# Third products of the delta rule's inverse by transposes, grouped exponentials, 42 slots and other planner durations in a two-layer hybrid network

## The chip, the cores and the metric

The kernel runs on one core of a Trainium2 chip. The metric is device time in microseconds (us): the median of several executions, from the first to the last instruction with what lies around them. A profile comes from one execution of its own.

## What is computed

A network of two layers on x of shape [256, 1024] in float32. Each layer is a SwiGLU feed-forward block (FFN, hidden width 2816), a mixer, and a second FFN; behind each stands a layer norm (LN) over the scaled residual. The mixer of layer 0 joins a gated delta rule (8 heads, chunks of 64) with an mLSTM (4 heads). The mixer of layer 1 is a chunked state-space model, SSD, with 32 heads in 4 groups.

```python
for l in range(DEPTH):
    x = layer_norm(DN_ALPHA * x + 0.5 * swiglu(x, pre_gate[l], pre_up[l], pre_down[l]))
    x = layer_norm(DN_ALPHA * x + (hybrid_mixer(x) if l % 2 == 0 else ssd_mixer(x)))
    x = layer_norm(DN_ALPHA * x + 0.5 * swiglu(x, post_gate[l], post_up[l], post_down[l]))
...
# delta rule, per head and chunk of 64
lower = jnp.where(strict, einsum('bhncd,bhnjd->bhncj', kb, k) * decay, 0.0)
sol = triangular_solve(lower + eye, rhs, left_side=True, lower=True)
...
# SSD, per chunk and head
seg = jnp.exp(jnp.where(causal, a_cum[..., :, None] - a_cum[..., None, :], -jnp.inf))
y_diag = einsum('bngcj,bngrcj,bnjgrp->bncgrp', cb, seg, xdt)
d_end = jnp.exp(a_cum[..., -1:] - a_cum)
```

## The kernel before, in words

**Matmuls in three parts.** Every weight arrives by DMA as a float32 tile `raw` (mostly 512 KB). ACT (ScalarE) casts it to a rounded `hi`, DVE (VectorE) writes `lo` = raw - hi, and the activations are split alike (`xh`, `xl`). A product is three matmuls: hi with xh, lo with xh, hi with xl. The FFNs take most of the span and are made of nothing else.

**An order written ahead.** No engine chooses its next instruction at run time. The whole network is first recorded as operations in a `Plan`. `Plan.rank` gives each a due time from TensorE's (PE's) sequence, `Plan.order` walks through modelled time and puts them in a fixed sequence for each of the five queues (PE, DVE, ACT, POOL, SP; SP issues the DMAs), and `Plan.emit` writes the instructions out. So almost every row of the profile has one line, that of the emitting loop (L488). The durations of the model are in `_cost`; `HAND` and `LAG` are delays between engines, `MARGIN` a reserve for DMAs of weights; `order` also models the row of DMAs and charges ACT for a change of its function table. `plan.group()` makes one operation of several calls, `plan.behind(op)` holds an operation behind another in the plan alone.

**Buffers.** SBUF tiles come from pools: `m4` (40 slots of 128 x 1040 floats) holds raw, hi, lo and most large tiles; `m2`, `m1` and the `tiny` ones are smaller. PSUM's 8 banks have three kinds: `acc` 4, `gu` 2, `tr` 2.

**Delta rule.** `Ls` (one tile per half of the sequence) holds the lower triangles. Their 16 x 16 diagonal blocks go through a scratch array in DRAM (`scrdl`) into `ab`; `block_inverse` inverts them on DVE, with constants for a 16 x 16 identity and a strict lower triangle, and its results return through DRAM as `T` (transposed inverse) and `U` (inverse). Two levels (`lv` 0: 16 to 32 rows; `lv` 1: 32 to 64) then grow them, in 4 steps for each level (two halves, two quads `q`). A step computes YZ from U and Ls, then corrects `uu` (U) with T·YZ and `tt` (T) with YZ·T, each by four matmuls into PSUM and a subtraction on DVE. While the blocks are on their way, PE works at the projections of the hybrid mixer and at the mLSTM, whose outputs `my` it transposes (`tr<-ident,my`).

**SSD.** For each of four groups, `decays` builds two tiles `abc` (one for each half, 128 x 1024): a DMA from scratch, 8 Relu on ACT, one exponential; and `sde`, a small exponential. The convolution's outputs `cv` go through Silu on ACT (to `bf`, `cf`, `xf`), the gate `zs` too; Exp and Silu are in different function tables, and each change is an ACT_TABLE_LOAD. `xe` (DVE) and `hst` (ACT) feed the products of the states.

Of the kernel before, what the change touches and what calls it, by code (L numbers as in the profile page):

```python
# [12 lines left out]
F32 = mybir.dt.float32  # L13
# [19 lines left out]
NSLOT = 40  # L33
# [7 lines left out]
C_EYE16 = 896  # L41
C_LOW16 = 1152
C_N = 1408


def _const_array():
    i = np.arange(P)[:, None]
    j = np.arange(P)[None, :]
    c = np.zeros((P, C_N), np.float32)
    c[:, C_NEG:C_NEG + P] = np.where(i <= j, 0.0, -BIG)  # L50
    c[:, C_POS:C_POS + P] = np.where(i <= j, 0.0, BIG)
    for n, s in enumerate((16, 32)):
        c[:, C_LEV + n * P:C_LEV + n * P + P] = (i // (2 * s) == j // (2 * s)) & (i % (2 * s) < s) & (j % (2 * s) >= s)
    c[:, C_PAIR:C_PAIR + P] = i // 64 == j // 64
    c[:, C_CAU:C_CAU + P] = i <= j
    c[:, C_LOW16:C_LOW16 + 256] = np.tril(np.ones((16, 16), np.float32), -1).reshape(1, 256)
    c[:, C_EYE16:C_EYE16 + 256] = np.eye(16, dtype=np.float32).reshape(1, 256)
    return c


SB_SLOTS = {"m4": (NSLOT, WMAX), "m2": (6, 512), "m1": (6, 256), "tiny": (12, 16), "tiny96": (12, 96)}
# [12 lines left out]
class Buf:  # L74


    def __init__(self, n, tag, shape, dtype, name):
# [6 lines left out]
        self.ops = []  # L84
        self.place = None
# [99 lines left out]
class Plan:  # L185
# [83 lines left out]
    def _cost(self, op, method, a, k):  # L269
# [12 lines left out]
        elif q == "SP":  # L282
# [5 lines left out]
            op.rate = 410 if isinstance(src, bass.AP) and not src.tensor.name.startswith("scr") else 300  # L288
        else:
# [20 lines left out]
            elif q == "ACT":  # L310
                op.busy += 180 + .85 * n + 60 * scal - LAG["ACT"] + (186 if "accum_out" in k else 0)
# [38 lines left out]
    MARGIN, LEAD = 1000, 0  # L350
# [3 lines left out]
    def order(self):  # L354
# [18 lines left out]
        dma = 0.0  # L373
# [12 lines left out]

        def start(o, q):
            t = max(ready[o, q], clock[q])
            if o.news:
# [23 lines left out]
        while len(out) < len(ops):  # L413
            best = None
            for q in QUEUES:
# [4 lines left out]
                now = [(o.prio + 2 * switch(o, q), o.n, t, o) for t, o in can if t <= t0]  # L420
                mine = min(now)
                for p, n, t, o in sorted((o.prio + 2 * switch(o, q), o.n, t, o) for t, o in can if t > t0):
# [34 lines left out]
            o.done, o.begun, o.on = end, t, q  # L457
            out.append(o)
# [32 lines left out]
class Net:  # L491
# [92 lines left out]
    def consts(self):  # L584
# [7 lines left out]
        self.ones = self.one([32, S], F32, name="ones")  # L592
        nc.gpsimd.memset(self.ones, 1.0)
# [277 lines left out]
    def hyb(self, g, b, last=False):  # L871
# [24 lines left out]
        ones = self.ones[0:8]  # L896

# [38 lines left out]
        with hp():  # L936
            sin = t96(12, "sin")
            V.tensor_copy(sin[:, :, 0:8], gt[:, :, 8:16])
            V.tensor_scalar_mul(sin[:, :, 8:12], gt[:, :, 20:24], -1.0)
# [147 lines left out]
        mq = self.m4([P, 2, S], nm="mq")  # L1087
# [3 lines left out]
        mk = self.m4([P, 2, S], nm="mk")  # L1091
# [3 lines left out]
        for pr in range(2):  # L1095
            for q in range(2):
# [64 lines left out]
        with hp():  # L1161
# [8 lines left out]
            for lv in range(2):  # L1170
# [112 lines left out]
    def block_inverse(self, ab, c, dd):  # L1283
# [4 lines left out]
        eye3 = c[:, C_EYE16:C_EYE16 + 256].rearrange("p (a b) -> p a b", a=16)  # L1288
        V.tensor_mul(ab, ab, c[:, C_LOW16:C_LOW16 + 256].rearrange("p (a b) -> p a b", a=16))
# [57 lines left out]
    def ssd(self, g, b, last=False):  # L1347
# [17 lines left out]
        ones = self.ones[:, 0:P]  # L1365
# [25 lines left out]
        V.tensor_copy(flat(dt), sp)  # L1391
# [7 lines left out]
        rw = self.m1([NH, S], nm="srow")  # L1399
        ds_ = [self.scratch([NH, P], f"ds{half}") for half in range(2)]  # L1400
# [16 lines left out]
        def decays(gi):  # L1417
            for half in range(2):
# [10 lines left out]
                A.activation(bc, bc, AF.Exp, scale=-1.0)  # L1429
                M[gi, half] = bc  # L1430

# [143 lines left out]
def _layouts(i):  # L1575
    f = lambda a: np.ascontiguousarray(np.asarray(a))
    o = {"cst": _const_array(), "ident": np.eye(P, dtype=np.float32), "x": f(i["x"])[0]}
# [59 lines left out]
```

## Time and profile before

| | |
|---|---|
| median of 3 runs | 1147.33 us (1146.54 to 1148.89) |
| profiled execution, its own time | 1146.67 us |
| its span, first to last instruction | 1144.9 us |
| PE busy, of the span | 1112.7 us, 97% |
| DVE busy | 758.5 us, 66% |
| ACT busy | 587.9 us, 51% |
| mean granted TensorE clock | 0.995 |

What happens in the profiled execution is told in its own time; 1.8 us of it lie outside the span. Busy shares are means over stages with different limits. The stages by the span's clock: FFN to 182 us, hybrid mixer to 376, two FFNs with an LN between them to 730, SSD to 970, the last FFN to the end.

### The profile page before, as it was taken

Reading aid. Unit: us, or ns where it says so; the run is one execution under the profiler, and the core shown is the slowest. Engines: PE = TensorE matmul, PEld = TensorE weight load, DVE = VectorE, ACT = ScalarE, POOL = GpSimd, SP = SyncE. Lnnn points to the kernel's source line nnn. Section 1 sums busy time; section 2 is a strip of 40 time slices with the busy share of each in tenths; the row PEclk is TensorE's granted clock in tenths of the full one; section 3 lists DMA queues with packets and bytes.
Section 4 is the critical chain, followed back from the end, with each engine's and each line's share of the span. In section 5 each row is a group of like instructions: output and inputs, shape, how many; then the busy total and the mean of one; then the engine's idle time right before and its main releaser. Section 6 shows DMA issues by size and latency. Waiting matters only on the chain.

```text
span 1144.9 us, 19783 instructions
## 1 busy us (share of the span) xinstructions
PE 1112.7 (97%) x8118; PEld 1041.5 (91%) x8118; DVE 758.5 (66%) x1242; ACT 587.9 (51%) x890; POOL 26.2 (2%) x53
## 2 busy tenths in 40 slices
PE   7999999998999999999999999999999999999996
PEld 7999998998998999999899999899998779999995
DVE  6945456787969955455865545696788889655425
ACT  6755443593423544344354444379889636444410
POOL 0000000000000000000000000000011220000000
PEclk9999999998999999999999999999999999999999
DMA  9766554648424555565465555465545446655601
GB/s 358 288 212 205 196 183 133 191 171 214 186 102 159 197 190 192 191 206 174 148 223 200 188 197 187 134 217 187 185 146 178 149 163 243 218 172 187 212 19 37
DMA packets 75955, 210.02 MB, mean 183 GB/s; under 512 B 13580, under 2 KB 26328, under 8 KB 75864
## 3 DMA queue, kind: packets, MB, share of 16 engines
q1 hardware_dynamic: 75864, 208.76, 54.3%
q8 instruction: 63, 1.03, 0.4%
q14 instruction: 28, 0.23, 0.1%
HBM read 204.23 MB, written 4.50 MB: 182 GB/s over the span
## 4 chain that ended last, share of the span: by engine, by line
PE 81%; DVE 8%; ACT 6%; DMA 3%; issue 1%; SPq 0%; DVEq 0%; ACTq 0%
PE gu L488 46%; PE acc L488 32%; PE tr L488 3%; DVE cv L488 2%; DMA raw<-in_wgu 2%; DVE lo L488 2%; ACT L488 2%; ACT abc L488 1%; DVE x L488 1%; ACT cv L488 1%; DMA ab<-scrdl 1%; ACT Ls L488 1%; ACT hi L488 0%; DVE ry L488 0%; DMA x<-in_x 0%
## 5 line engine op out<-in xcount | busy, mean ns | idle before, releaser
L488 DVE TENSOR_TENSOR lo<-raw,hi 128x1024 fp32r<-128x1024 f32 (+2 forms) x358 | 428.8, 1216 | 145.0 <-ACT hi L488 141.4
L488 ACT CAST hi<-raw 128x1024 fp32r<-128x1024 f32 (+2 forms) x358 | 370.1, 1045 | 203.0 <-DMA raw<-in_wgu 125.1
L488 PE MATMUL gu<-xl,hi 128*128 128x256 f32 x1216 | 341.9, 281 | 0.0
L488 PE MATMUL gu<-xh,hi 128*128 128x256 f32 x1216 | 341.2, 281 | 0.0
L488 PE MATMUL gu<-xh,lo 128*128 128x256 f32 x1216 | 341.1, 281 | 0.0
L488 PEld LDWEIGHTS gu<-xh,hi 128*128 128x128 f32 x1216 | 229.0, 188 | 1.0
L488 PEld LDWEIGHTS gu<-xl,hi 128*128 128x128 f32 x1216 | 228.9, 188 | 1.1
L488 PEld LDWEIGHTS gu<-xh,lo 128*128 128x128 f32 x1216 | 229.1, 188 | 0.0
L488 PE MATMUL acc<-hi,h 128*128 128x512 f32 (+1 forms) x748 | 228.7, 381 | 0.0
L488 PEld LDWEIGHTS acc<-hi,h 128*128 128x128 f32 x748 | 138.1, 188 | 27.5
L488 PE MATMUL acc<-lo,h 128*128 128x512 f32 (+1 forms) x374 | 142.1, 380 | 0.0
L488 ACT ACTIVATE sg<-gu 128x256 f32<-128x256 f32 (+1 forms) x100 | 35.9, 359 | 183.3 <-PE gu L488 183.1
L488 DVE TENSOR_TENSOR hf<-sg,gu 128x256 f32<-128x256 f32 (+1 forms) x100 | 38.7, 388 | 108.2 <-ACT sg L488 108.0
L488 PE MATMUL acc<-xh,hi 128*128 128x256 f32 x320 | 92.7, 290 | 0.0
L488 PE MATMUL acc<-xl,hi 128*128 128x256 f32 x320 | 90.5, 283 | 0.0
L488 PE MATMUL acc<-xh,lo 128*128 128x256 f32 x320 | 90.2, 282 | 0.0
L488 PEld LDWEIGHTS acc<-lo,h 128*128 128x128 f32 x374 | 70.3, 188 | 13.1
L488 PE MATMUL acc<-hi,xh 128*128 128x260 f32 x224 | 64.0, 286 | 0.0
L488 PE MATMUL acc<-hi,xl 128*128 128x260 f32 x224 | 63.4, 283 | 0.4 <-DVE xl L488 0.4
L488 PE MATMUL acc<-lo,xh 128*128 128x260 f32 x224 | 63.3, 283 | 0.0
L488 PEld LDWEIGHTS acc<-xh,hi 128*128 128x128 f32 x320 | 61.0, 190 | 0.6 <-issue 0.2
L488 DVE TENSOR_TENSOR h<-hf,h 128x256 fp32r<-128x256 f32 x76 | 32.3, 425 | 44.0 <-ACT h L488 44.0
(272 smaller groups left out, 1445.5 us busy)
## 6 DMA issues: line engine op xcount, KB each, us to landing
raw<-in_wgu SPq DMA_DIRECT2D x176, 512.0 KB, 5.0
raw<-in_wd SPq DMA_DIRECT2D x88, 512.0 KB, 5.8
raw<-in_ssd_fm SPq DMA_DIRECT2D x24, 512.0 KB, 5.7
raw<-in_ssd_tm SPq DMA_DIRECT2D x16, 520.0 KB, 4.5
raw<-in_hyb_fm SPq DMA_DIRECT2D x16, 512.0 KB, 5.2
raw<-in_ssd_out SPq DMA_DIRECT2D x16, 512.0 KB, 5.7
raw<-in_hyb_tm SPq DMA_DIRECT2D x12, 520.0 KB, 4.4
raw<-in_hyb_out SPq DMA_DIRECT2D x8, 512.0 KB, 6.8
```

The source lines that it names most:

```text
L488: getattr(engines[o.on], method)(*map(real, a), **{x: real(v) for x, v in k.items()})
```

## The change

- `m4` has 42 slots instead of 40. To make room, the constants lose their two 16 x 16 tables (1408 to 896 columns), which become an array of their own, `cst16`, read by DMA into an `m2` tile `c16` (128 x 512, 256 KB) shortly before `block_inverse`; a shared tile `ones` is replaced by two short-lived ones, `mq` and `mk` share one tile, and `tiny96` shrinks.
- The planner's numbers are others: DMA rates and latencies, `MARGIN` 1500 instead of 1000, `LATE` 200, 40 more for an ACT operation with a scalar operand outside PSUM, and a rule that an operation waits for another engine's last use of its PSUM bank.
- In `decays`, the 16 Relus of a group of heads come first, and then all its exponentials as one planned operation.
- In the delta rule's two levels, the four matmuls of YZ·T and the DVE subtraction are replaced by four transposes of `uu` on PE and one copy on ACT into `tt`.

```diff
-NSLOT = 40
+NSLOT = 42
...
-SB_SLOTS = {"m4": (NSLOT, WMAX), "m2": (6, 512), "m1": (6, 256), "tiny": (12, 16), "tiny96": (12, 96)}
+SB_SLOTS = {"m4": (NSLOT, WMAX), "m2": (6, 512), "m1": (6, 256), "tiny": (12, 16), "tiny96": (11, 64)}
...
-            op.rate = 410 if isinstance(src, bass.AP) and not src.tensor.name.startswith("scr") else 300
+            far = [v for v in (out, src) if isinstance(v, bass.AP)][0]
+            if far.tensor.name.startswith("scr"):
+                piece = 4 * far.ap[-1][1]
+                op.rate = 82 if piece <= 64 else 228 if isinstance(src, View) else 291
...
-    MARGIN, LEAD = 1000, 0
+    SWITCH = 2
+    MARGIN, LATE, LEAD = 1500, 200, 0
...
+            for b in o.banks:
+
+                for e, end in b.seen.items():
+                    if e != q:
+                        t = max(t, end + HAND[e][q])
...
-                first = max(dma, t + busy)
-                dma = first + max(350, o.bytes / o.rate)
-                end = dma + 2000 + self.MARGIN * o.raw
+                took = max(350, o.bytes / o.rate)
+                row = 1 if t + busy >= dma else row + 1
+                dma = max(t + busy + 2100 + took, dma + took + (1300 if row == 2 and took > 900 else 0))
+                end = dma + self.LATE
...
+        c16 = self.m2([P, 512], nm="c16")
+        with self.plan.behind(qk):
+            DQ(c16, self.ap["cst16"])
         with hp():
-            self.block_inverse(ab, c, dd)
+            self.block_inverse(ab, c16, dd)
...
                         V.tensor_sub(cut(uu[:, sl], 1), cut(uu[:, sl], 1), cut(v3(p1), 1))
-                        if lv == 0:
-                            for k in range(4):
-                                T.matmul(p2[:, k * P:k * P + P], yz[:, 4 * q + k, :], tt[:, 4 * q + k, :], start=True, stop=True)
-                            V.tensor_sub(cut(tt[:, sl], 0), cut(tt[:, sl], 0), cut(v3(p2), 0))
-                        else:
-                            for k in range(4):
-                                T.matmul(p2[0:64, k * 64:k * 64 + 64], yz[:, 4 * q + k, 0:64], tt[:, 4 * q + k, 0:64], start=True, stop=True)
-                            V.tensor_sub(tt[32:64, sl, 0:32], tt[32:64, sl, 0:32], v3(p2[32:64, 0:S])[:, :, 0:32])
+                        n = P if lv == 0 else 64
+                        for k in range(4):
+                            T.transpose(p2[0:n, k * n:k * n + n], uu[0:n, 4 * q + k, 0:n], ident[0:n, 0:n])
+                        A.copy(tt[0:n, sl, 0:n], v3(p2[0:n, 0:4 * n]))
...
                 if half == 0:
-                    sl = slice(gi * 8, gi * 8 + 8)
                     V.tensor_add(de[:, sl], bc[:, :, P - 1], nam[:, 0, sl])
-                    A.activation(de[:, sl], de[:, sl], AF.Exp)
-                    V.tensor_mul(de[:, sl], de[:, sl], dt[:, 0, sl])
                 for r in range(8):
                     h = gi * 8 + r
                     A.activation(bc[:, r, :], bc[:, r, :], AF.Relu, scale=-1.0, bias=pam[:, half, h:h + 1])
-                A.activation(bc, bc, AF.Exp, scale=-1.0)
                 M[gi, half] = bc
+            with self.plan.group():
+                if gi == 0:
+                    A.activation(ea, nam[:, 1, :], AF.Exp, scale=-1.0)
+                A.activation(de[:, sl], de[:, sl], AF.Exp)
+                for half in range(2):
+                    A.activation(M[gi, half], M[gi, half], AF.Exp, scale=-1.0)
+            V.tensor_mul(de[:, sl], de[:, sl], dt[:, 0, sl])
```

The order of the FFNs' matmuls on PE is unchanged. Three places where it moves follow; a row is one instruction, or several alike (x4), with the tile written, the tiles read and the columns.

First, PE in the hybrid mixer where the mLSTM's outputs `my` are transposed; `acc_3168` and `acc_3163` are the same projection, whose matmuls follow. Before:

```order
L488 MATMUL tr_3118<-mv_339_1966,mE_2662 128x129 x2
L488 MATMUL tr_3123<-mv_339_1966,mE_2740 128x129 x2
L488 MATMUL tr_3133<-mv_339_1966,mE_2662 128x129 x4
L488 MATMUL tr_3145<-ident,my_3141 128x128
L488 MATMUL tr_3148<-mv_339_1966,mE_2740 128x129
L488 MATMUL tr_3145<-ident,my_3141 128x128
L488 MATMUL tr_3148<-mv_339_1966,mE_2740 128x129 x2
L488 MATMUL tr_3145<-ident,my_3141 128x128 x2
L488 MATMUL tr_3148<-mv_339_1966,mE_2740 128x129
L488 MATMUL acc_3168<-xh,hi_2877 128x256
L488 MATMUL acc_3168<-xl,hi_2877 128x256
```

And with the change:

```order
L507 MATMUL tr_3120<-mv_339_1952,mE_2669 128x129 x2
L507 MATMUL tr_3124<-mv_339_1952,mE_2734 128x129 x2
L507 MATMUL tr_3132<-mv_339_1952,mE_2669 128x129 x4
L507 MATMUL tr_3146<-mv_339_1952,mE_2734 128x129 x4
L507 MATMUL acc_3163<-xh,hi_2843 128x256
L507 MATMUL acc_3163<-xl,hi_2843 128x256
L507 MATMUL acc_3163<-xh,lo_2916 128x256
L507 MATMUL acc_3163<-xh,hi_2843 128x256
L507 MATMUL acc_3163<-xl,hi_2843 128x256
L507 MATMUL acc_3163<-xh,lo_2916 128x256
L507 MATMUL tr_3173<-ident,my_3157 128x128 x4
```

Four of the mLSTM's matmuls and six of the projection now stand ahead of the first transpose of `my`. On SP, the read of `c16` now stands between the two reads of `ab`, where before one read of a weight stood; on ACT, the first exponential of `Ls` and its table load no longer stand between `kf` and the squares `sq`.

Second, PE in the second half's first level and the start of the second level. Before:

```order
L488 MATMUL gu_3608<-YZ_2342,T_2324 128x128 x4
L488 MATMUL tr_3615<-T_2324,YZ_2342 128x128 x4
L488 MATMUL gu_3622<-YZ_2342,T_2324 128x128 x4
L488 MATMUL tr_3632<-T_2324,YZ_2342 128x128 x4
L488 MATMUL gu_3638<-U_2298,Ls_2580 128x128 x4
L488 MATMUL gu_3646<-U_2298,Ls_2580 128x128 x4
```

And with the change:

```order
L507 MATMUL gu_3600<-YZ_2326,T_2261 128x128 x4
L507 MATMUL gu_3596<-U_2289,Ls_2696 128x128 x2
L507 MATMUL gu_3610<-U_2245,Ls_2633 128x128 x2
L507 MATMUL tr_3614<-ident,U_2289 128x128 x4
L507 MATMUL gu_3620<-YZ_2326,T_2261 128x128 x4
L507 MATMUL gu_3610<-U_2245,Ls_2633 128x128 x2
L507 MATMUL gu_3632<-U_2245,Ls_2633 128x128 x3
L507 MATMUL tr_3638<-ident,U_2289 128x128 x4
```

Before, both products of a step stood next to each other; now the transposes of U stand behind four to five matmuls of another step.

Third, ACT at SSD's first group of heads. Before:

```order
L488 ACTIVATE abc_8430<-abc_8430,spam 128x128
L488 ACT_TABLE_LOAD
L488 ACTIVATE sde<-sde 128x8
L488 ACTIVATE cv_8615<-acc_8518,scw 128x256
L488 ACTIVATE cv_8624<-acc_8518,scw 128x256
L488 ACTIVATE abc_8430<-abc_8430 128x1024
L488 ACTIVATE abc_8442<-abc_8442,spam 128x128 x3
L488 ACT_TABLE_LOAD
L488 ACTIVATE cf_8668<-cv_8615 128x256
```

And with the change:

```order
L507 ACTIVATE abc_8447<-abc_8447,spam 128x128 x8
L507 ACTIVATE abc_8449<-abc_8449,spam 128x128 x8
L507 ACT_TABLE_LOAD
L507 ACTIVATE sea<-sam 128x32
L507 ACTIVATE sde<-sde 128x8
L507 ACTIVATE abc_8447<-abc_8447 128x1024
L507 ACTIVATE abc_8449<-abc_8449 128x1024
L507 ACTIVATE cv_8618<-acc_8451,scw 128x256
L507 ACTIVATE cv_8621<-acc_8451,scw 128x256
```

All sixteen Relus and four exponentials now stand ahead of the next `cv`; over the whole program ACT's order holds 22 table loads instead of 38, of which 10 instead of 24 are in SSD.

## Rows read from the trace of the kernel before

**Rows 1.** The page, busy time of each engine.

```profile
PE 1112.7 (97%) x8118; PEld 1041.5 (91%) x8118; DVE 758.5 (66%) x1242; ACT 587.9 (51%) x890; POOL 26.2 (2%) x53
```

**Rows 2.** Windows: busy PE, PEld, DVE, ACT, POOL; PEclk; DMA share; GB/s.

```profile
270.00:376.00 106.00, 100.76 (x771) 92.34 (x772) 88.41 (x204) 39.17 (x59) 0.00 (x0) 0.97 0.48 155
...
730.00:970.00 240.00, 232.02 (x1662) 213.89 (x1661) 196.38 (x331) 172.80 (x291) 23.36 (x40) 1.00 0.53 178
```

**Rows 3.** Waits of PE: total us, times, longest us.

```profile
PE tr L488 <- DVE my L488: 4.5, 1, 4.5
PE gu L488 <- DVE xe L488: 2.7, 2, 1.7
PE gu L488 <- ACT hst L488: 2.7, 3, 1.9
PE tr L488 <- ACT cf L488: 1.8, 2, 1.5
```

**Rows 4.** Timeline of PE at `my`: start us, us, operation, idle before.

```profile
267.47 1.95 PE L488 MATMUL tr<-mv,mE 128*128 128x129 f32 x16
273.91 0.45 PE L488 MATMUL tr<-ident,my 128*128 128x128 f32 x1 [4.49 <-DVE my L488]
```

**Rows 5.** Windows around that wait, columns as in rows 2.

```profile
268.70:274.00 5.30, 0.81 (x8) 0.65 (x6) 5.13 (x15) 1.04 (x1) 0.00 (x0) 0.84 0.17 18
274.00:279.00 5.00, 5.00 (x24) 5.00 (x25) 3.36 (x17) 0.59 (x1) 0.00 (x0) 0.50 0.89 187
```

**Rows 6.** Timeline of DVE ahead of `my`.

```profile
251.51 1.11 DVE L488 SCALAR_TENSOR_TENSOR Ls<-tr,rkkb,Ls 128x128 f32<-128x128 f32 x4
...
264.26 0.43 DVE L488 TENSOR_TENSOR ab<-ab,cst 128x256 f32<-128x256 f32 x1 [2.25 <-DMA ab<-scrdl]
...
273.41 0.61 DVE L488 SCALAR_TENSOR_TENSOR my<-tr,md,sg 128x128 f32<-128x128 f32 x2
```

**Rows 7.** Timeline of ACT between `kf` and `sq`.

```profile
241.00 1.28 ACT L488 ACT_TABLE_LOAD   x1
242.29 1.06 ACT L488 ACTIVATE Ls<-Ls 128x1024 f32<-128x1024 f32 x1
```

**Rows 8.** Groups of PE, 182 to 376 us: busy us, mean ns, idle before.

```profile
L488 PE MATMUL tr<-T,YZ 128*128 128x128 f32 x32 | 4.3, 278 | 0.0
...
L488 PE MATMUL tr<-T,YZ 128*64 128x64 f32 x32 | 2.7, 228 | 0.0
```

**Rows 9.** Timeline of PE in the delta rule.

```profile
309.13 1.06 PE L488 MATMUL tr<-T,YZ 128*128 128x128 f32 x8
310.02 1.06 PE L488 MATMUL gu<-U,Ls 128*128 128x128 f32 x8
310.92 0.60 PE L488 MATMUL tr<-ident,vf 128*128 128x128 f32 x4
```

**Rows 10.** Groups of DVE, 300 to 342 us.

```profile
L488 DVE TENSOR_TENSOR U<-U,gu 128x256 f32<-128x256 f32 x8 | 3.3, 418 | 3.7 <-PE gu L488 3.6
...
L488 DVE TENSOR_TENSOR T<-T,tr 128x256 f32<-128x256 f32 x4 | 1.7, 415 | 0.4 <-PE tr L488 0.4
```

**Rows 11.** Groups of ACT, 182 to 376 us.

```profile
L488 ACT CAST hi<-raw 128x1024 fp32r<-128x1024 f32 x37 | 38.2, 1049 | 21.9 <-DVE lo L488 8.8 <-DMA raw<-in_hyb_fm 8.3 <-DMA raw<-in_wgu 4.2
```

**Rows 12.** Groups of ACT in SSD, 730 to 970 us.

```profile
L488 ACT ACT_TABLE_LOAD x24 | 30.8, 1283 | 2.4 <-DVE cv L488 2.1
L488 ACT ACTIVATE abc<-abc,spam 128x128 f32<-128x128 f32 x64 | 20.2, 392 | 0.7 <-DVE sde L488 0.7
...
L488 ACT ACTIVATE abc<-abc 128x1024 f32<-128x1024 f32 x8 | 8.5, 1058 | 0.1
```

**Rows 13.** Timeline of ACT ahead of the longest `hst` wait.

```profile
830.86 1.28 ACT L488 ACT_TABLE_LOAD   x1
832.16 1.06 ACT L488 ACTIVATE abc<-abc 128x1024 f32<-128x1024 f32 x1
833.12 0.57 ACT L488 COPY hst<-gu 128x512 f32<-128x512 f32 x1
```

More of the change, by code (lines that the diff above doesn't have):

```diff
@@ L40 @@
 C_PAIR = 768
-C_EYE16 = 896
-C_LOW16 = 1152
-C_N = 1408
+C_N = 896
 def _const_array():
@@ L55, in _const_array, with _const16 @@
     c[:, C_CAU:C_CAU + P] = i <= j
-    c[:, C_LOW16:C_LOW16 + 256] = np.tril(np.ones((16, 16), np.float32), -1).reshape(1, 256)
-    c[:, C_EYE16:C_EYE16 + 256] = np.eye(16, dtype=np.float32).reshape(1, 256)
-    return c
-SB_SLOTS = {"m4": (NSLOT, WMAX), "m2": (6, 512), "m1": (6, 256), "tiny": (12, 16), "tiny96": (12, 96)}
+    return c
+def _const16():
+    c = np.stack([np.eye(16, dtype=np.float32), np.tril(np.ones((16, 16), np.float32), -1)])
+    return np.broadcast_to(c.reshape(1, 512), (P, 512)).copy()
+SB_SLOTS = {"m4": (NSLOT, WMAX), "m2": (6, 512), "m1": (6, 256), "tiny": (12, 16), "tiny96": (11, 64)}
 PS_SLOTS = {"ps": 8}
@@ L84, in __init__ @@
         self.ops = []
+        self.seen = {}
         self.place = None
@@ L310, in _cost @@
             elif q == "ACT":
-                op.busy += 180 + .85 * n + 60 * scal - LAG["ACT"] + (186 if "accum_out" in k else 0)
+                op.busy += 180 + .85 * n + 60 * scal - LAG["ACT"] + (40 if scal and not ps else 0) + (186 if "accum_out" in k else 0)
                 f = a[2] if method == "activation" and len(a) > 2 else None
@@ L372, in order @@
         clock["SP"] = 700.0
-        dma = 0.0
+        dma, row = 0.0, 0
         table = None
@@ L385, in order @@
                 offer(o)
+        for o in ops:
+            o.banks = list({v.buf for _, a, k in o.calls for v in list(a) + list(k.values())
+                            if isinstance(v, View) and v.buf.psum})
         def start(o, q):
             t = max(ready[o, q], clock[q])
+            for b in o.banks:
+                for e, end in b.seen.items():
+                    if e != q:
+                        t = max(t, end + HAND[e][q])
             if o.news:
@@ L419, in order @@
                 t0 = max(min(t for t, _ in can), clock[q] + 1)
-                now = [(o.prio + 2 * switch(o, q), o.n, t, o) for t, o in can if t <= t0]
+                now = [(o.prio + self.SWITCH * switch(o, q), o.n, t, o) for t, o in can if t <= t0]
                 mine = min(now)
-                for p, n, t, o in sorted((o.prio + 2 * switch(o, q), o.n, t, o) for t, o in can if t > t0):
+                for p, n, t, o in sorted((o.prio + self.SWITCH * switch(o, q), o.n, t, o) for t, o in can if t > t0):
                     if p + self.WAIT * (t - t0) < mine[0] and t - t0 < self.FRAC[q] * mine[3].busy:
@@ L457, in order @@
             o.done, o.begun, o.on = end, t, q
+            for b in o.banks:
+                b.seen[q] = end
             out.append(o)
@@ L591, in consts @@
         self.x = self.one([P, 2, D], F32, name="x")
-        self.ones = self.one([32, S], F32, name="ones")
-        nc.gpsimd.memset(self.ones, 1.0)
         self.mhalf = self.one([P, 1], F32, name="mhalf")
@@ L955, in hyb @@
             rw = self.m4([8, 4, S], nm="hrows")
+            ones = self.m1([8, S], nm="ones")
+            with self.plan.behind(neg):
+                G.memset(ones, 1.0)
             for half in range(2):
@@ L1090, in hyb @@
         A.copy(flat(mq), ps)
-        mk = self.m4([P, 2, S], nm="mk")
+        mk = mqk[:, 2:4]
         ps = self.acc()
@@ L1399, in ssd @@
         rw = self.m1([NH, S], nm="srow")
+        ones = self.m1([NH, P], nm="ones")
+        with self.plan.behind(soft):
+            G.memset(ones, 1.0)
         ds_ = [self.scratch([NH, P], f"ds{half}") for half in range(2)]
@@ L1417, in decays @@
         def decays(gi):
+            sl = slice(gi * 8, gi * 8 + 8)
             for half in range(2):
@@ L1576, in _layouts @@
     f = lambda a: np.ascontiguousarray(np.asarray(a))
-    o = {"cst": _const_array(), "ident": np.eye(P, dtype=np.float32), "x": f(i["x"])[0]}
+    o = {"cst": _const_array(), "cst16": _const16(), "ident": np.eye(P, dtype=np.float32), "x": f(i["x"])[0]}
     gu, dn = [], []
```

17 lines of the change are left out of this document (7 added, 10 removed).

## The prediction, made before the changed kernel ran

> **What bounds the kernel now.** I read the busy times first. PE is busy for 1112.7 us [rows 1] of a span of 1144.9, so it waits for 32.2 us in all; whatever the change does, it acts through those 32.2 us, through the work on PE itself, or through TensorE's clock. The windows say where the waits lie: 5.2 us in the stretch with the delta rule (106.00 less 100.76) and 8.0 us in SSD (240.00 less 232.02) [rows 2]; in SSD DVE is busy for 196.38 of 240 us and ACT for 172.80 [rows 2], so DVE is the fuller of the two. The waits of PE name who ends them: the longest of those in reach of the change is one of 4.5 us for DVE's `my`; in SSD they are `xe` (DVE, longest 1.7), `hst` (ACT, longest 1.9) and `cf` (ACT, longest 1.5) [rows 3].
>
> The wait for `my` costs more than its length. PE's last matmul ahead of it is done at 269.4 and the transposes begin at 273.91 [rows 4]. In the stretch with the wait the granted clock is 0.84, and in the 5 us behind it 0.50, the lower level of 1.2 GHz [rows 5]: PE is busy for all 5.00 us and does what 2.5 us do at the full 2.4 GHz. So this wait costs 4.5 + 2.5 = 7.0 us. The `hst` wait of 1.9 us let nothing fall: SSD's clock is 1.00 [rows 2]. Between idle times of 1.9 and 4.5 us lies the point at which the clock is lost.
>
> What makes `my` late is on DVE. Its multiplications into `Ls` end at 252.6; the blocks go to DRAM and back, DVE fills the time with casts and sits idle for 2.25 us before `ab` arrives at 264.26; the block inverse follows, and `my` starts at 273.41 [rows 6].
>
> **The change, part by part.**
>
> *The wait for `my` (planner).* Three edits meet here. First, the exponential of the first `Ls` and its table load, 1.28 + 1.06 us [rows 7], no longer stand ahead of the squares `sq` on which DVE's multiplications wait; three Relus of 0.32 each (the Relus of SSD have the same shape: 20.2 us for 64 [rows 12]) take their place, so `Ls` is done about 2.34 - 0.95 = 1.4 us earlier, and `ab` lands at about 262.9. The read of `c16` (256 KB) between the two reads of `ab` replaces one of 512 KB, so it should not delay them; at worst, if it is itself late, the block inverse starts where it does now. Second, DVE has more to do behind `Ls`: before, 252.6 to 262.0 were 9.4 us of work; by the order six masks (on `gbc` and `mE`) and a copy move there. The masks have the shape of the `Ls` multiplications, 0.28 us each, one or two of them double: 1.9 us; the copy has that of `ab`'s first operation, 0.4 [rows 6]. From 251.2 this ends at 251.2 + 11.7 = 262.9, when `ab` lands too. With 0.4 us for what slips, `ab` starts at 263.3 in place of 264.26, and `my` comes about 0.9 us earlier, at 272.5; PE can transpose its first tile at 273.0, and with all four tiles in one piece I take 273.2. Third, PE arrives later: eight more records of mv·mE at 0.11 us (1.95 us for 16 [rows 4]) and six matmuls of the projection at 0.12, 0.9 + 0.7 = 1.6 us, are done before the wait and not after it. PE then stops at 271.05 and waits 2.1 us (1.4 to 3.3, by how much of the 1.4 us arrives). Gain: 1.6 + 0.7 = 2.3 us, and 2.5 more if 2.1 us of idle time keep the clock. Nearer to 1.9 than to 4.5, it should: 4.8 us. The bounds are 0.7 (nothing but an earlier `my`) and 7.0.
>
> *Third products by transposes.* Before, a step issues four matmuls in float32, which the trace counts as two records each: eight records of 128 columns go by in 310.02 - 309.13 = 0.89 us [rows 9]. Four transposes take one record each: the transposes of `vf` are four in 0.60 us, the last record's 0.28 included, so 0.11 apart [rows 9], 0.44 us for four. Level 0 has 32 records [rows 8], so 4 steps each save 0.44 us: 1.8 us. Level 1's 32 records of 64 columns [rows 8] have half the columns and save half, 0.9 us. Together 2.7 us of PE, in a stretch where PE hardly waits (5.2 us of idle time in 106, 4.5 of them for `my` [rows 2, 3]). DVE loses its subtractions (four of 0.415 us, four smaller [rows 10]); ACT gains eight copies, of 0.57 us for 128 x 512 by the copy of `hst` [rows 13]. What is new is a chain: T now follows U, whose subtraction on DVE takes 0.418 us [rows 10], before the transposes can start; four or five matmuls of another step stand ahead of most of them (0.9 to 1.1 us), which covers that at level 0. At the end of level 1 the matmuls in between are of 64 columns and cover half as much; I put the uncovered part at 1.0 us. Net gain: 1.7 us, between 0.5 (each of the eight steps uncovered by 0.3) and 2.7.
>
> Here a rule of the Trainium skill speaks against the change. "TensorE: Matmul & The Clock Gate", Part 4, says that transposes do not count as TensorE work for the full clock. This trace does not bear it out so far: the transposes of `vf` go by at 0.107 us each, as fast as matmuls of 128 columns [rows 9], and the 2.5 us lost behind `my` with the fall ahead of it are all that takes this stretch from 1.00 to 0.97 [rows 2, 5]. By the rule the sum would lose its 2.7 us and more, which is the fourth rival.
>
> *Grouped exponentials.* SSD has 24 table loads of 1283 ns, 30.8 us [rows 12]; 14 go, 18.0 us of ACT's time. But ACT is idle for 67 of its 240 us and PE waits on it there for 2.7 + 1.8 us [rows 3], so nearly all of it is hidden under PE's projections. What it can reach: ahead of the longest `hst` wait ACT did a load and an exponential, 1.28 + 1.06 us [rows 13]; with the exponentials done earlier that wait shrinks by some 0.7 us. Against that, 16 Relus (5.1 us), a load, two exponentials of 1.06 us and two small ones stand in one row ahead of the next `cv` (about 9 us), so the wait for `cf` should stay at 1.5. DVE's list in SSD is the same as before, 82% full, and sets `xe`: what PE gains at `hst` it mostly waits for at the next `xe`. I take 0.5 us for SSD as a whole; the bounds are 4 us (half of its idle time) and -3 (a `cf` wait of 4.5).
>
> The Trainium skill, "ScalarE: Activation LUTs", section "What ACT_TABLE_LOAD costs", adds a drain of about 1.38 us to each load, 2.66 us in all; by that, 14 loads would be 37 us of ACT and not 18. The trace shows none: a load from 241.00 takes 1.28 us, and the exponential starts at 242.29 [rows 7].
>
> *The rest.* 42 slots let two more weight tiles be under way; PE waits for no weight in the list of waits but through ACT and DVE, so I take nothing (up to 1 us). The reserve of 1500 only moves the order; the FFNs, whose order on PE is unchanged, keep their time. Layer norms and the ends: 0, at most 0.5 either way.
>
> **The sum.** 4.8 + 1.7 + 0.5 = 7.0 us. From the profiled execution's own 1146.67 us that gives 1139.7. That execution lies 0.66 us below the median of the runs, so the forecast for the median is 1140.3 us.
>
> **Rivals.**
>
> 1. *The first wait gives little, or it is given back.* The clock falls all the same (2.3 instead of 4.8), or PE, now 4 us ahead of DVE, waits for it later in the delta rule and the LN; the covers there fail (0.5 to 0.9). For it: DVE is busy for 88.41 of 106 us [rows 2] and gains only 0.9 us at `my`. Against it: DVE waited 3.6 us for PE's `gu` in the delta rule [rows 10], so it has slack. 2.3 + 0.9 + 0 = 3.2 us: 1144.1.
> 2. *All waits go.* `my` is there in time (2.3 + 2.1 + 2.5 = 6.9), the transposes cost nothing (2.7), and SSD loses half of its idle time (4.0): 13.6 us, 1133.7. For it: ACT has 18 us to give back. Against it: DVE's fullness in SSD.
> 3. *Slower: the rows of exponentials hold up ACT.* About 9 us on ACT in one piece, four times, ahead of `cv`, `cf` and `xf`. If PE's wait for `cf` or `xe` grows from 1.5 to 4.5 us it costs 3.0 and, as behind `my`, the clock: 2.5 more. Two such places cost 11 us and leave 1140.3 + 0.5 + 11 = 1151.8; one leaves 1146.3, no change. It decides from the point where one idle time passes somewhere between 1.9 and 4.5 us at two places. Against it: ACT's idle 67 us.
> 4. *Slower: transposes let the clock fall.* The stretch of the two levels is about 25 us; at 0.50 it costs 12.5 us: 1140.3 + 12.5 = 1152.8. Against it: rows 9, above.
> 5. *The copies of T are late.* ACT's casts `hi` there wait for DVE's `lo` 8.8 us in all [rows 11]; a copy behind such a cast waits with it. If half of the eight copies lose 1 us, the term is 1.7 - 4: 1144.3.
>
> **Chances and range.** The forecast 0.45 (its own range, 1137.5 to 1142.5, from the bounds of its terms); rival 1 0.25; rival 2 0.12; rival 3 0.09; rival 4 0.02; rival 5 0.07. A measurement of this kernel tells 0.2% from no change, 2.3 us: faster is below 1145.0. Rival 1 is so in about two of three cases and rival 5 in five of seven; the rest of both, and 0.02 of rival 3, is no change. Faster 0.45 + 0.17 + 0.12 + 0.05 = 0.79; same 0.08 + 0.02 + 0.02 = 0.12; slower 0.07 + 0.02 = 0.09. The range leaves out rivals 3 and 4 and most of rival 2 on its low side: 1134.5 to 1147.
>
> **What would show it.** Right: PE's wait for `my` is 1.4 to 3.3 us and no window behind it shows 0.50; the two levels issue 2.7 us less, with waits of PE for DVE's U or ACT's T of about 1 us; ACT holds 22 loads; SSD's idle time is 7 to 8 us, with `xe` as its largest part. Wrong: a clock of 0.50 anywhere in the mixers; a wait of over 3 us for `cf` or `xe`; a new wait of PE for `hi` or `lo` in the FFNs.

## The result and the profile after

The changed kernel takes 1133.18 us in the median of four runs (1131.81 to 1134.58), beside 1147.77 (1146.54 to 1148.89) before: a ratio of 0.987 with the interval 0.986 to 0.989, 14.6 us faster. The forecast was 1140.3 and its range 1134.5 to 1147: the direction was right, the size was not.

The profiled execution took 1134.58 us with a span of 1132.8. First the page's busy times, then the windows of [rows 2] (busy PE, PEld, DVE, ACT, POOL; PEclk; DMA share; GB/s):

```profile
PE 1107.6 (98%) x8086; PEld 1036.0 (91%) x8086; DVE 753.8 (67%) x1234; ACT 573.1 (51%) x882; POOL 25.8 (2%) x54
```

```profile
270.00:376.00 106.00, 103.03 (x802) 93.90 (x801) 89.79 (x204) 46.90 (x76) 0.00 (x0) 1.00 0.51 164
730.00:970.00 240.00, 235.82 (x1718) 219.17 (x1717) 201.44 (x336) 158.02 (x281) 22.78 (x40) 1.00 0.56 187
```

PE waits for 25.2 us in all instead of 32.2, and is busy for 5.1 us less. The waits of PE after, beside [rows 3]:

```profile
PE tr L507 <- DVE y L507: 2.5, 2, 1.6
PE tr L507 <- DVE x L507: 1.7, 3, 0.9
PE tr L507 <- ACT bf L507: 1.1, 2, 0.9
PE tr L507 <- DVE my L507: 0.8, 1, 0.8
PE gu L507 <- DVE xe L507: 0.6, 1, 0.6
```

`my` is waited for 0.8 us instead of 4.5, `hst` and `cf` no longer at all. PE's and DVE's timelines at `my`, beside [rows 4, 6], and the window behind the wait, beside [rows 5]:

```profile
267.88 2.84 PE L507 MATMUL tr<-mv,mE 128*128 128x129 f32 x24
272.21 0.95 PE L507 MATMUL tr<-ident,my 128*128 128x128 f32 x3 [0.78 <-DVE my L507]
```

```profile
250.31 1.11 DVE L507 SCALAR_TENSOR_TENSOR Ls<-tr,rkkb,Ls 128x128 f32<-128x128 f32 x4
...
262.61 0.42 DVE L507 TENSOR_TENSOR ab<-ab,c 128x256 f32<-128x256 f32 x1
...
271.71 0.61 DVE L507 SCALAR_TENSOR_TENSOR my<-tr,md,sg 128x128 f32<-128x128 f32 x2
```

```profile
272.00:280.00 8.00, 7.66 (x63) 7.32 (x64) 7.39 (x20) 2.65 (x5) 0.00 (x0) 1.00 0.91 195
```

DVE no longer sits idle ahead of `ab`; `Ls` is done at 251.4 (forecast 251.2), `ab` starts at 262.6 (263.3), `my` at 271.7 (272.5), and the clock stays at 1.00.

To compare stages I take the start of the last transposes of x (`tr<-ident,x`) in each layer norm as its end. From one such mark to the next, in us of each profiled execution:

```
                    LN1 to LN3   LN3 to LN4   SSD (LN4 to LN5)   PE idle in SSD
before                  358.50       189.16             201.68              8.0
changed                 350.90       189.10             196.34              4.2
```

LN1 to LN3 is the mixer of layer 0 with the FFN behind it (7.6 us shorter); the mixer's own end (LN2) moves in the order, so the FFN is taken with it. SSD is 5.3 us shorter; 3.8 of that is PE's idle time. The rest, 0.65 us longer ahead of LN1 and 0.3 behind LN5, brings this to 12.1 us of the span. The other 2.5 us between the medians lie between executions: the profiled one of before is among its fastest, that of the changed kernel is its slowest, and the last section shows a likely cause.

### The profile page after: what moved, and what is told of

It is laid out like the page before. It is cut to its first block, busy times and chain, and to the rows that moved or that the text cites. A ratio compares the mean times of both kernels' runs of the same rounds, so it can differ in the third digit from the quotient of the medians.

```text
span 1132.8 us, 19754 instructions
## 1 busy us (share of the span) xinstructions
PE 1107.6 (98%) x8086; PEld 1036.0 (91%) x8086; DVE 753.8 (67%) x1234; ACT 573.1 (51%) x882; POOL 25.8 (2%) x54
## 4 chain that ended last, share of the span: by engine, by line
PE 85%; DVE 7%; DMA 3%; ACT 3%; issue 1%; SPq 0%; DVEq 0%; ACTq 0%
PE gu L507 46%; PE acc L507 36%; PE tr L507 3%; DMA raw<-in_wgu 2%; DVE lo L507 1%; DVE x L507 1%; DMA raw<-in_hyb_out 1%; DVE cv L507 1%; ACT abc L507 1%; DMA abc<-scrds 1%; ACT hi L507 1%; ACT L507 0%; DVE Ls L507 0%; DVE ry L507 0%; ACT Ls L507 0%
## 5 line engine op out<-in xcount | busy, mean ns | idle before, releaser
L507 PEld LDWEIGHTS acc<-xl,hi 128*128 128x128 f32 x320 | 60.3, 189 | 0.2 <-issue 0.2
```

Of the source, the lines that this page charges most:

```text
L507: getattr(engines[o.on], method)(*map(real, a), **{x: real(v) for x, v in k.items()})
```

## The experiments

### One part alone on the kernel before

The planner's hunks alone (`_cost`, `rank`'s constants, `order`):

```diff
-    MARGIN, LEAD = 1000, 0
+    SWITCH = 2
+    MARGIN, LATE, LEAD = 1500, 200, 0
...
+            for b in o.banks:
...
```

> The kernel before with the planner's numbers alone (no further slots, no transposes, no grouped exponentials). Its order at the transposes of my is that of the changed kernel: four matmuls and six of the projection ahead, sq two loads earlier. Theory A (the planner's numbers end the wait for my): the wait is 0.5 to 1.5 us, no window behind it shows a clock of 0.50, and the mixer of layer 0 is some 5.6 us shorter, while SSD keeps its time within 1.5 us: about 1142. Rival B (the planner's numbers also make SSD's gain): SSD is 4 to 6 us shorter too, about 1137. Rival C (the read of c16 or the further slots end the wait): my waits 3 us or more and the time stays at 1146 to 1148.

Measured: 1138.25 us, ratio 0.990 [0.989, 0.992]. SSD takes 195.28 us and PE waits there for 2.2 us: rival B of the expectation, the planner's numbers make SSD's gain too. Its window from LN4 to LN5, then PE's waits:

```profile
751.00:946.30 195.30, 193.11 (x1403) 178.67 (x1402) 162.58 (x268) 151.88 (x259) 23.58 (x40) 1.00 0.55 186
```

```profile
PE tr L505 <- DVE ri L505: 2.8, 1, 2.8
PE tr L505 <- DVE my L505: 1.8, 1, 1.8
PE gu L505 <- DVE xe L505: 1.8, 1, 1.8
```

The first of them is new: in the LN behind the mixer (LN2), where the next FFN's matmuls no longer stand between the transposes.

One wait of SSD shows how the order alone ends it. Before, the longest wait for `hst` had a table load and an exponential on ACT that began 0.8 us after PE's product for `hst` was done (830.86 [rows 13], 830.09 in the trace); `hst` followed at 833.12. With the planner's numbers alone, ACT at the same place:

```profile
823.18 1.28 ACT L505 ACT_TABLE_LOAD   x1
824.48 2.00 ACT L505 ACTIVATE abc<-abc 128x1024 f32<-128x1024 f32 x2
```

Here the load is over before that product is done (825.28), `hst` follows at 826.39, and PE does not wait for it. The other waits of SSD were not followed in this way.

The transposes alone:

```diff
-                                T.matmul(p2[:, k * P:k * P + P], yz[:, 4 * q + k, :], tt[:, 4 * q + k, :], start=True, stop=True)
...
+                            T.transpose(p2[0:n, k * n:k * n + n], uu[0:n, 4 * q + k, 0:n], ident[0:n, 0:n])
...
```

> The kernel before with the third products by transposes alone. Theory A (2.7 us of TensorE work less, hardly any of it given back): the stretch from the first U,Ls product to the first vr,U product is 1.9 to 2.7 us shorter, the wait for my and its clock of 0.50 stay: 1145. Rival (the copies of T on ACT are late): it is 0 to 1 us shorter, 1147. Rival (transposes let the clock fall): a window of 0.50 between 300 and 330 us.

Measured: 1151.01 us, 1.0016 [1.0005, 1.0028], a little slower. Up to the first transpose of `o` the delta rule is 4.1 us shorter, more than the 2.7 expected, but the order behind it is another one, and LN2 has the same new wait as above. PE's timeline at this wait and at `hst` in SSD, then a window behind each:

```profile
367.49 0.63 PE L488 MATMUL tr<-ident,x 128*128 128x128 f32 x4 [2.85 <-DVE ri L488]
...
836.64 1.22 PE L488 MATMUL gu<-hst,cf 128*128 128x512 f32 x1 [1.76 <-ACT hst L488]
```

```profile
368.00:372.00 4.00, 4.00 (x23) 3.90 (x22) 3.83 (x12) 1.53 (x2) 0.00 (x0) 0.58 0.02 6
836.00:840.00 4.00, 3.36 (x11) 2.33 (x12) 3.79 (x6) 3.69 (x7) 0.32 (x2) 0.57 0.00 0
```

The wait for `hst` is that of before in kind and length (1.9 us [rows 3]); here the clock fell behind it.

The grouped exponentials alone:

```diff
-                A.activation(bc, bc, AF.Exp, scale=-1.0)
...
+            with self.plan.group():
...
+                A.activation(de[:, sl], de[:, sl], AF.Exp)
+                for half in range(2):
+                    A.activation(M[gi, half], M[gi, half], AF.Exp, scale=-1.0)
```

> The kernel before with the grouped exponentials alone: 24 table loads in place of 38. Theory A (ACT's loads stood in the chains to xe and hst, since DVE's idle time in SSD ends on ACT): SSD, from the LN ahead of it to the LN behind it, is 3 to 5.5 us shorter, hst is no longer waited for, and DVE's waits for ACT's cv, abc and sde shrink by 10 us in sum: 1143. Rival B (SSD is bound by DVE, and the gain there came from the planner's numbers or the further slots): SSD is 0 to 1 us shorter, 1147.

Measured: 1151.37 us, 1.0017 [1.0005, 1.0029]. Both theories missed: SSD is 4.3 us longer (206.03). PE's waits there and a window behind the second:

```profile
884.45 0.63 PE L488 MATMUL tr<-ident,y 128*128 128x128 f32 x4 [1.25 <-DVE sde L488]
889.74 1.19 PE L488 MATMUL gu<-xe,btm 128*128 128x512 f32 x1 [3.06 <-ACT hi L488]
```

```profile
890.00:902.00 12.00, 12.00 (x44) 9.65 (x43) 7.39 (x11) 3.54 (x5) 0.00 (x0) 0.50 0.01 1
```

The trace names ACT's `hi`, but PE starts right behind the end of `xe` (889.59 in DVE's trace). This is rival 3 of the prediction: a longer wait for `xe`, and twelve microseconds at 1.2 GHz behind it. PE's idle time in SSD is less than before, 6.1 us and not 8.0: the one long wait, with the clock behind it, makes the stage longer.

### One part taken out of the changed kernel

> The changed kernel with the planner's old numbers (42 slots, transposes and grouped exponentials stay). Theory A (the planner's numbers alone gave 5 us at my and 6 us in SSD; the other three parts give little without them): PE waits 4 to 5 us for my with a clock of 0.50 behind it, SSD takes 200 us or more from LN to LN, and the time is 1143 to 1150. Rival B (slots, transposes and group give a gain of their own): 1140 or less.

With the planner's old numbers: 1149.94 us, 1.0006 [0.9992, 1.002]. Slots, transposes and group together are worth nothing without them; SSD takes 207.04 us, with a wait of 3.05 us for `xe`.

> The changed kernel with the old third products (four matmuls and a subtraction on DVE). Theory A (2.7 us of TensorE work, 2.1 of them kept): the stretch from the first U,Ls product to the first transpose of o is 1.7 to 2.7 us longer than in the changed kernel, everything else within 1 us: 1135 to 1136. Rival (an order of its own elsewhere decides, as in the kernel before, where the transposes alone brought a longer wait at the LN): a wait of over 2 us or a clock of 0.50 in another stage, 1138 or more.

With the old third products: 1132.44 us, 0.986 [0.983, 0.988], not to be told from the changed kernel. The delta rule up to the first transpose of `o` is 2.0 us longer, as expected; at LN2 0.5 us less is waited for x and nothing for `hf`, and at LN3 the difference is 0.5 us.

> The changed kernel without the grouped exponentials (the old decays), 34 table loads. Theory A: SSD is 3 to 5.5 us longer than in the changed kernel, hst and xe are waited for again: 1138. Rival B (the planner's numbers and the slots give SSD's gain without the group): within 1 us, 1134.

With the exponentials apart, 34 loads: 1133.45 us, 0.988 [0.986, 0.991], the same too. Its profiled execution has a `cf` wait of 3.0 us and SSD at 201.31, theory A's picture. But that execution is the slowest of four (1132.58 to 1137.64), and whether the other three had this wait is not on record; in the median it does not show.

> The changed kernel with 40 slots and the old constants. Theory (slots are worth nothing that can be measured): 1132.5 to 1135. Rival (two more weights under way cover waits in SSD or at the FFNs): 1136 or more.

With 40 slots and the old constants: 1146.99 us, 0.999 [0.998, 1.000]. The gain is gone: the time is the rival's, but the waits below come from the order of the queues, not from weights that are late. DVE's timeline ahead of the third `xe`, ACT's, and PE's:

```profile
879.22 2.36 DVE L505 TENSOR_TENSOR abc<-abc,cb 128x1024 f32<-128x1024 f32 x2 [0.55 <-ACT abc L505]
881.50 0.69 DVE L505 TENSOR_TENSOR y<-tr,svec 128x512 f32<-128x512 f32 x1
882.95 0.69 DVE L505 TENSOR_TENSOR syl<-tr,syh 128x512 fp32r<-128x512 f32 x1 [0.77 <-ACT syh L505]
883.56 0.68 DVE L505 TENSOR_TENSOR xe<-tr,sde 128x512 f32<-128x512 f32 x1
```

```profile
870.43 4.80 ACT L505 ACTIVATE abc<-abc,spam 128x128 f32<-128x128 f32 x16
875.14 1.00 ACT L505 ACTIVATE cv<-acc,scw 128x256 f32<-128x256 f32 x2
...
878.14 1.99 ACT L505 ACTIVATE abc<-abc 128x1024 f32<-128x1024 f32 x2
...
882.34 1.06 ACT L505 CAST syh<-tr 128x512 fp32r<-128x512 f32 x2
```

```profile
879.24 1.04 PE L505 MATMUL tr<-ident,xf 128*128 128x128 f32 x8
...
884.38 1.19 PE L505 MATMUL gu<-xe,btm 128*128 128x512 f32 x1 [4.11 <-ACT hi L505]
```

The trace names ACT's `hi`, but PE starts 0.14 us after `xe` ends (883.56 + 0.68), so `xe` it is. Its inputs were there at 880.3; it stands in DVE's queue behind both `abc` and behind `syl`, which waits for the cast `syh`, which stands on ACT behind the whole row of Relus and exponentials. The wait of 4.1 us, and the 4 us lost in the window behind it, are about the 8.5 us by which SSD (203.74) is longer than with the planner's numbers alone (195.28):

```profile
885.00:893.00 8.00, 8.00 (x26) 5.79 (x24) 6.46 (x9) 2.77 (x4) 0.00 (x0) 0.50 0.00 0
```

### Pairs

> The kernel before with the planner's numbers and the 42 slots with their smaller constants; old third products, exponentials apart. Theory A (these two parts are the gain; the transposes' 2 us are waited away at the LN behind the mixer, and the group is worth nothing in this order): 1132 to 1135, with no wait over 2 us in any stage and no clock of 0.50 ahead of the last layer norm. Rival B (the group is needed for SSD): SSD is 200 us or more, 1137 or more.

Planner's numbers and slots: 1133.67 us, 0.988 [0.986, 0.990]: the whole gain. SSD 196.80, LN1 to LN3 351.06. Ahead of LN2's last transposes the next FFN's matmuls are back; the longest wait in its mixers is one for `xe`, of 1.2 us:

```profile
PE gu L507 <- DVE xe L507: 2.7, 3, 1.2
PE tr L507 <- DVE my L507: 0.7, 1, 0.7
```

> The kernel before with the planner's numbers and the grouped exponentials (40 slots, old products). Theory A (the row of 16 Relus and the exponentials ahead of a cast that DVE waits for makes PE wait at xe, whatever the products are): SSD is 200 to 206 us, where the planner's numbers alone gave 195.3, with a wait of 3 us or more for xe and a clock of 0.50 behind it; 1143 to 1148. Rival B (in the run with 40 slots it was the transposes): SSD 194 to 197 us, 1138.

Planner's numbers and group, 40 slots: 1145.61 us, 0.998 [0.996, 0.999]. SSD 201.05, with a wait of 4.57 us for `xe`: the group lengthens SSD there without the transposes (theory A).

> The kernel before with the planner's DMA numbers alone (rates, latencies, MARGIN, LATE), without the rule on PSUM banks and ACT's 40. Its order has sq earlier, as the changed kernel, but only one matmul of mv,mE more ahead of my. Theory A (sq earlier and work moved ahead are two separate shares of the gain at my): my waits 2 to 4 us, the clock falls behind it, half of the gain there. For SSD: rival B (DMA numbers give its gain) 194 to 197 us, rival C (ACT's durations and the banks give it) 200 to 203.

> The kernel before with the planner's rule on PSUM banks and ACT's 40 alone, the old DMA numbers (40 slots, nothing else). Its order puts three matmuls of mv,mE ahead of my, and sq stays late. Theory A (SSD's gain comes from these two, since ACT's casts and convolutions are what its waits end on): SSD 194 to 198 us, my waits 3 us or more with the clock's fall: about 1143. Rival B (SSD's gain needs both, or it is the DMA numbers in this sum): SSD 200 us or more, 1146 or more.

The DMA numbers alone: 1146.57 us, 0.998 [0.997, 1.000]; SSD 204.87. The rule on banks with ACT's 40: 1145.78 us, 0.998 [0.996, 1.000]; SSD 205.38. Each half makes the stretch of `my` shorter by some 4 us up to the first transpose of `qf`; in these executions neither shortens SSD. In the first, `my` is waited for 2.72 us and, against the expectation, the clock stays; in the second the wait for `xe` is 1.88 us, and it falls:

```profile
272.42 0.50 PE L493 MATMUL tr<-ident,my 128*128 128x128 f32 x2 [2.72 <-DVE my L493]
```

```profile
271.00:280.00 9.00, 7.58 (x64) 7.49 (x65) 8.14 (x28) 2.23 (x3) 0.00 (x0) 1.00 0.91 198
```

```profile
886.34 1.10 PE L500 MATMUL gu<-xe,btm 128*128 128x512 f32 x2 [1.88 <-DVE xe L500]
```

```profile
887.00:896.00 9.00, 9.00 (x39) 8.43 (x38) 5.14 (x7) 6.98 (x11) 0.83 (x3) 0.52 0.08 30
```

For the second this hangs on the clock. Its window from LN4 to LN5 has 4.9 us of idle time on PE, where before there were 8.0; but PE is busy for 6.8 us more than before (193.7), at a clock of 0.96:

```profile
751.80:957.20 205.40, 200.52 (x1404) 185.50 (x1403) 163.38 (x269) 151.67 (x260) 20.62 (x40) 0.96 0.52 177
```

Its ten runs lie from 1141.53 to 1150.66 us, and the profiled one (1148.92, mean clock 0.988) is among the slowest; the fastest has a mean clock of 0.994. So in this execution the rule on banks with ACT's 40 does shorten the waits of SSD, by 3 us of the 5.8 that both halves take away (8.0 to 2.2), and loses it here through the clock. The DMA numbers alone leave 7.7 us of waits.

### One wait or one resource, with the order kept

The kernel before, its wait for `my` partly filled:

```diff
+                for i in range(getattr(o, "warm", 0)):
...
+                    nc.tensor.matmul(o.news[0].place[:, 0:256], xh[:, i % 8, 0:128], xh[:, i % 8, :], start=True, stop=True)
```

> The kernel before, with 24 further matmuls of 128x256 from xh into the tile that the first transpose of my then overwrites, ahead of that transpose; order and everything else as before, results unchanged. They take 2.8 us of the 4.5 us in which PE waits. Theory A (the wait cost 2.5 us through the clock on top of its 4.5): no window of 0.50 behind it, and the time falls by 2.5 us to about 1145. Rival (the clock's fall comes from something else or costs nothing on the path): the same time, 1147.5.

Measured: 1148.2 us, 0.9992 [0.998, 1.0003]. The 2.2 us that were left idle were enough for the clock to fall:

```profile
269.01 3.12 PE L493 MATMUL tr<-xh 128*128 128x256 f32 x24
274.35 0.33 PE L495 MATMUL tr<-ident,my 128*128 128x128 f32 x1 [2.22 <-DVE my L495]
```

```profile
275.00:279.00 4.00, 4.00 (x24) 4.00 (x23) 3.47 (x15) 0.59 (x1) 0.00 (x0) 0.57 0.82 181
```

So it did not measure what it was made for. The next one did:

```diff
...
+        back = [i for i in range(my[0]) if order[i].on == "PE"][-5:]
+        moved = [order[i] for i in back]
+        order = [o for i, o in enumerate(order[:my[3] + 1]) if i not in back] + moved + order[my[3] + 1:]
```

> The changed kernel with the last four matmuls of mv,mE and the six matmuls of the projection put back behind the four transposes of my. Theory A (the wait was covered by 1.6 us of work moved ahead and by an earlier my): PE waits 2.4 us in place of 0.8, the clock stays at 1.00, 1.6 us longer than the changed kernel: 1135. Rival (2.4 us of idle time let the clock fall): a window of 0.50 and 4 us longer, 1137.5.

Measured: 1136.21 us, 0.990 [0.988, 0.992], 3.0 us above the changed kernel. The wait is 2.35 us and the clock falls, as the rival said, for less than it gave:

```profile
271.48 0.50 PE L513 MATMUL tr<-ident,my 128*128 128x128 f32 x2 [2.35 <-DVE my L513]
```

```profile
272.00:276.00 4.00, 3.89 (x20) 3.82 (x21) 2.11 (x11) 0.59 (x1) 0.00 (x0) 0.57 0.79 131
```

1.57 us more of waiting and 1.7 us lost at half the clock (4 x 0.43) are 3.3 us; from LN1 to the first transpose of `qf` this execution is 3.0 us longer than that of the changed kernel (80.3 to 77.3). Work moved ahead of this wait is worth its length, and the clock besides.

Table loads put back:

```diff
+                    if hasattr(o, "mark") and i >= len(o.calls) - 2:
+                        nc.scalar.activation(o.mark.real(), o.mark.real(), AF.Silu)
...
```

> The changed kernel with a small Silu (128x8, into a tile that nobody reads any more) ahead of each of the two large exponentials of a group: 16 table loads and eight small operations more on ACT, 38 loads in all; the order of every other instruction on every engine is unchanged. Theory A (ACT's loads end the chains of SSD): each group is 5 to 6 us later on ACT, and SSD is 4 us or more longer than in the changed kernel: 1138 or more. Rival B (loads are hidden in SSD, and the order alone gave the gain): within 1 us, 1134.

Measured: 1167.56 us, 1.017 [1.015, 1.019], 34 us above the changed kernel. SSD of this run, and of the changed kernel (windows from LN4 to LN5):

```profile
746.20:977.10 230.90, 206.33 (x1403) 189.24 (x1402) 163.07 (x269) 159.56 (x273) 21.27 (x40) 0.91 0.47 156
```

```profile
746.90:943.30 196.40, 192.22 (x1404) 178.20 (x1403) 162.56 (x269) 136.79 (x249) 22.78 (x40) 1.00 0.55 184
```

ACT works 22.8 us more; PE waits 24.6 us instead of 4.2, and the remaining 14 of 34.5 us are the same matmuls at a mean clock of 0.91. ACT is busy for 70% of SSD in the changed kernel and still has no slack where these loads stand. In the run with the exponentials apart 12 more loads cost nothing in the median; there the order was planned with them, which may be why, but no run isolates it.

One DVE instruction moved in the kernel with 40 slots:

```diff
...
+        i, j = order.index(abc), order.index(xe)
+        i = max([i] + [order.index(d) + 1 for d in xe.deps])
...
+        order.insert(i, order.pop(j))
```

> The kernel of the run with 40 slots, with one DVE instruction moved: the third group's xe stands ahead of the second multiplication of abc and of syl, which waits for ACT's cast behind the row of exponentials; every other instruction keeps its place. Theory A (there PE's wait of 4.1 us for xe and the clock of 0.50 behind it are the price of a row of exponentials ahead of a cast that DVE waits for in order): the wait is 1 us or less, no window of 0.50 follows it, SSD is 5 to 8 us shorter than the 203.7 of that run: about 1140. Rival B (something else, such as a weight's DMA or ACT's hi, ends that wait, or PE waits as long at the next place): SSD stays at 202 or more, 1146.

Measured: 1144.13 us, 0.996 [0.995, 0.998], 2.9 us less than its own base. The wait for `xe` is 0.92 us, so its place in the queue was the cause. But PE waits again at the next place, here beside DVE's row:

```profile
880.55 1.10 PE L518 MATMUL gu<-xe,btm 128*128 128x512 f32 x2 [0.92 <-DVE xe L518]
883.74 0.47 PE L518 MATMUL gu<-xd,abc 128*128 128x64 f32 x2 [2.10 <-ACT hi L518]
```

```profile
882.31 0.69 DVE L518 TENSOR_TENSOR syl<-tr,syh 128x512 fp32r<-128x512 f32 x1 [0.17 <-ACT syh L518]
882.91 0.68 DVE L518 TENSOR_TENSOR xd<-tr,sdt 128x512 f32<-128x512 f32 x1
```

This matmul reads `xd` and `abc`. The second `abc` is done at 881.54, `xd` at 883.59, 0.15 us ahead of the matmul: it is `xd` that PE waits for now, and `xd` still stands behind `syl`.

Theory A holds for the wait, rival B for what follows: SSD is 201.55, 2.2 us shorter and not 5 to 8.

## Why the prediction was wrong

**The wait for `my`: right, a little small.** 4.8 us were forecast. From LN1 to the first transpose of `qf` it is 83.2 us before and 77.3 after: 5.9. PE stops at 271.4 (forecast 271.05), `my` is 0.8 us earlier than forecast, and the wait is 0.8 us and not 2.1. So the 2.5 us for the clock came true by the shorter wait and not as reasoned: behind 2.1 us the clock would have been a coin's toss (last section). The planner's numbers do most of it (a wait of 1.8 us in that run); the kernels with `c16` and 42 slots have `my` another 0.7 to 1.6 us earlier than those with 40 and the new numbers.

**Third products: the term was 1.7, the path keeps at most 0.5 of it.** The delta rule up to `o` is 2.1 us shorter, within the forecast's range, and no wait for U or T appears, where 1.0 us was allowed for. (The range's lower end was mis-added: 2.7 less eight times 0.3 is 0.3, not 0.5.) But the two runs with planner's numbers, slots and old products (1132.44, 1133.67) are as fast as the two with transposes (1133.18, 1133.45). PE reaches LN2 earlier and waits there and in the FFN behind it: 1.6 us for x and `hf` from 330 us to LN3, instead of 0.5 in the two runs with the old products; at LN3 0.5 us is left. The prediction had this loss only in rival 1.

The Trainium skill's rule that transposes do not hold the full clock ("TensorE: Matmul & The Clock Gate", Part 4) does not show here: over both levels, where 32 transposes of `U` run, the granted clock is 1.00. Over 200 records of matmuls run among them, so this does not test the rule by itself.

```profile
296.00:324.00 28.00, 27.26 (x251) 24.49 (x250) 21.23 (x38) 12.17 (x22) 0.00 (x0) 1.00 0.24 79
```

**SSD: 0.5 was forecast, 5.3 measured; this step failed.** It read: "DVE's list in SSD is the same as before, 82% full, and sets `xe`: what PE gains at `hst` it mostly waits for at the next `xe`". DVE's work is the same and was no bound: with the planner's numbers alone PE's idle time in SSD is 2.2 us, and in the changed kernel 4.2 with 0.6 for `xe`, where 7 to 8 with `xe` as the largest part were forecast. SSD's gain was looked for in the grouped exponentials alone; the planner's numbers got no term there, though they reorder the same queues. They are the whole of it (SSD 195.28 with them alone, 196.34 with everything). The group shows no gain beside them and the slots: with and without it the medians are 1133.18 and 1133.45, with the old products 1132.44 and 1133.67. With 40 slots it makes SSD 4 to 9 us longer, by the mechanism of rival 3 at one place (waits of 3.1, 4.1 and 4.6 us for `xe`); with 42 slots and the old numbers the wait is 3.05.

The Trainium skill's rule to batch functions by table set ("ScalarE: Activation LUTs", "Table sets: the hidden batching unit") counts loads; here 34 loads and 22 gave the same time (1133.67 and 1133.18), and where the row of exponentials makes PE wait, it is by its place in ACT's queue (the kernel with 40 slots, above).

**The slots: nothing was forecast.** Under the planner's numbers the medians differ by 4.6 us (1138.25 to 1133.67), the ratios to the kernel before by less, some 3 us (0.9902 and 0.9877): `my` is earlier by 1.1, and LN2's wait of 2.85 us is gone with its clock. Beside the group and the transposes they are worth 13.8 us (1146.99 to 1133.18), in part since with 40 slots the row of exponentials costs its 4 to 9 us. With the old numbers they ran only together with the other two parts (1149.94), so their own worth there is not shown.

**The clock: one row taken for a bound.** "The `hst` wait of 1.9 us let nothing fall" was true of one execution. The last section shows that the clock falls behind such a wait in some executions, so the kernel before probably pays for its waits of 1.7 and 1.9 us in SSD in some runs and not in others; the changed kernel has none over 1.6 between its start and its end.

Put right, the terms of the profiled pair are 5.9 us for `my`, 1.7 from there to the end of the FFN behind (as much with the old products), and 5.3 for SSD, less 0.8 elsewhere: 12.1. The result is near rival 2's 1133.7 us, but not by rival 2's ways.

What stays open: which moves of the order make SSD's gain, beyond the one wait for `hst` followed above, and what the DMA numbers add there to the rule on banks. Nor is it shown which part of the slots' edit (the slots, the constants, the shared tiles) counts. Each run has one order, and no run isolates which of its many moves counts.

## What to carry to other kernels

With a static order made by a planner, changing the planner's numbers is a change of every stage: read the new order at each stage's longest wait, not only where the other edits are. A share of busy time does not say what bounds a stage; the instruction ahead of the late one in its queue does. A part that shortens an engine's work pays only if the next wait on that path gets shorter too, so follow its gain to the end of the stage before counting it.

## What the hardware did that was not expected

Whether TensorE's clock falls goes with how long PE sat idle, and not sharply. In the profiled executions of the 17 kernels here, away from the start and the end, no wait up to 1.66 us was followed by a fall, unless a longer wait came right behind it. Of the fifteen from 1.70 to 2.10 us six were (1.76 and 1.92 for `hst` in two runs, 1.88 for `xe`) and nine were not (1.92 for `hst` before, 1.97 for `my`). Of the 23 from 2.2 us up only one was not (2.72, above). A fall cost 1.5 to 7 us, worked out from the granted clock behind it.

The times of whole executions go with it. Of 77 further executions of the kernel before, 26 have the mean clock of the profiled one, 0.995, and a median of 1147.4 us; the nine with 0.990 to 0.992 have 1150.7. The changed kernel's four have 0.997 to 0.998. Where the clock fell in executions without a profile is not on record.
